# One more block group and one plain group less in both up projections, with a pinned order in the down projections

## The chip, the cores and the metric

The kernel runs on one core of one Trainium2 chip. The metric is the time of one execution on the device in microseconds; lower is better. The profile comes from one more execution of the same program, and its times count from the start of its span.

## The reference

A decoder trunk of two layers works on one sequence of 512 tokens with 1024 features, in float32. Layer 0 has an attention mixer, layer 1 a gated short convolution, and each layer ends with the same gated MLP, which is what the change touches:

```python
def conv_ffn(h, norm_g, w_up, conv_w, w_down):
    xn = rms_norm(h, norm_g)
    u = causal_dwconv(xn @ w_up, conv_w)      # width 3 along the tokens
    g, val = u[..., :D_FF], u[..., D_FF:]     # D_FF = 2816
    return (jax.nn.silu(g) * val) @ w_down
```

The up projection is 512 x 1024 times 1024 x 5632, the down projection 512 x 2816 times 2816 x 1024.

## The kernel before

**Precision.** Each float32 product is made of three matmuls on a fast float32 format. An operand is split into a high half `hi` (a copy by ScalarE into that format) and a low half `lo` (the rest, a subtraction on VectorE); hi x hi, hi x lo and lo x hi are summed in PSUM. So each block of weights that arrives costs one ScalarE copy (`whi`) and one VectorE subtraction (`wlo`) before TensorE can use it.

**Plain groups.** D_FF is cut into 22 column tiles of 128 for the gate and as many for the value; two neighbouring tiles make a group, of which there are `HF` = 11. The first `CLASSIC` = 3 groups of each MLP are multiplied plainly (`up_seven`, the loop over `j`): for each tile and each half (gate, value) `products` runs eight steps of three matmuls with 512 columns. They run on the activations before they are normalized, so this stage can start before the norm's row is known; `normed` multiplies the results by that row later.

**Block groups.** The other eight groups (class `Sevens`) use a seven-product scheme in the manner of Strassen: activations are cut into two halves of tokens and two of features, weights into four blocks of 512 x 256, and seven products of half size replace eight. `slot(g, s)` is one product of group `g` (24 matmuls with 256 columns, `seven`) with what is done beside it: weights are loaded (`load_pair`, `load_one`), summed on the way by accumulating transfers on the GpSimd queue (`add_block`) or by VectorE, split into halves (`weights_of`), and the results of the group before are joined, convolved, gated and multiplied (`tail`). The activations' seven forms are made once, by two runs of `prepare`, from the normalized rows.

**Chores.** Work that waits for the norm's row (`normed`, `prepare`, `gate_one`) is a list of generators. Between two steps of the plain stage, `work_off(SHARE)` gives the list a credit of 0.58 us and issues from it until the credit is used; each `yield` names a cost. What is left when the plain groups end is issued in the first block group, at 1.4 us per slot in its first four slots and without limit from the fifth on. `gate_one(g, i)` is the convolution (two VectorE taps for each half), SiLU and gate product of one tile of a plain group.

**Banks.** PSUM tiles have three tags: `a` (2 banks), `b` (4), `c` (2). A plain tile's gate half goes to `a`, its value half to `b`; block groups use `a` and `b`; the norm uses `c`.

**Down projection.** `mlp` runs 42 steps, seven phases (p1, p7, p2, p6, p3, q5, q4) over six groups of rows. Step `i` fetches the weights of step `i + 2`, multiplies, converts the activations of step `i + 2` (`operand`), and makes the block sums of step `i - 1` (`sums`). Weights of some phases are sums of two blocks: by accumulating transfers, or, for the last three groups of q5, by a second transfer into `other` and a VectorE sum (line 233).

**Order.** A scheduler orders the instructions of each engine ahead of time, by program order and by when it expects inputs to be ready; on the chip each engine but TensorE's weight loads takes its queue in that order. `tc.keep_in_program_order` ties an instruction behind the one traced just before it on its engine. Before the change it is used for the accumulating transfers and the `hi` copies of `weights_of`.

**The start.** `load(0)` brings the first 512 KB of attention weights in one transfer, queued on SyncE between the first and the second slice of x.

## Time and profile before

| | |
|---|---|
| median of 3 runs | 1135.77 us (1134.57 to 1136.08) |
| the profiled execution | 1138.21 us, span 1136.2 us |
| TensorE busy, share of the span | 1122.1 us, 99% |
| VectorE busy | 965.4 us, 85% |
| ScalarE busy | 670.3 us, 59% |
| first MLP: plain stage, block groups, down projection | from 278, 346.6 and 504 us |
| second MLP: the same | from 793, 861.7 and 1018 us |

How to read it: PE is TensorE, PEld its weight loads, DVE VectorE, ACT ScalarE, POOL GpSimd, SP SyncE. A timeline row gives the start and the duration in us, the engine, the line of the kernel, the operation, what it writes and reads, a count, and in brackets how long the engine was idle before it and what ended that. A row of windows gives a stretch, its length, busy time and count of each engine, then TensorE's granted clock, the transfer engines' share and GB/s.

### The profile page before, as it was taken

How to read it: one execution, taken by the hardware profiler on the slowest of the kernel's cores; microseconds unless marked ns; L12 is line 12 of the kernel's file. 1: busy time of each engine (PE TensorE's matmuls, PEld its weight loads, DVE VectorE, ACT ScalarE, POOL GpSimd, SP SyncE). 2: the span in 40 equal slices, each digit the busy share in tenths (PEclk: the TensorE clock that was granted, in tenths of full speed). 3: DMA queues.
4: the chain of work that ended last, by engine and by line, in shares of the span. 5: the costliest groups of instructions: out<-in, count | busy, mean ns of one | idle time of the engine just before them, and what ended most of it. 6: DMA issues, size and time to landing. Idle time of an engine off the chain costs nothing.

```text
span 1136.2 us, 19079 instructions
## 1 busy us (share of the span) xinstructions
PE 1122.1 (99%) x7547; PEld 1007.1 (89%) x7547; DVE 965.4 (85%) x1459; ACT 670.3 (59%) x999; POOL 133.0 (12%) x150
## 2 busy tenths in 40 slices
PE   8999999999999999999999999999999999999998
PEld 7888787878889999999999889988889999998886
DVE  6787888887899898989878888875798999889886
ACT  7556576755546767676547445544445766667553
POOL 4000000000012111014300001000001211014300
PEclk9999999999999999999999999999999999999999
DMA  6412212022366867689971655633375786789961
GB/s 192 112 38 75 57 39 74 26 87 75 106 182 118 191 160 163 172 235 194 224 185 31 172 118 142 130 111 93 93 195 112 167 191 137 181 220 216 230 168 56
DMA packets 160440, 155.31 MB, mean 137 GB/s; under 512 B 6396, under 2 KB 136492, under 8 KB 160352
## 3 DMA queue, kind: packets, MB, share of 16 engines
q1 hardware_dynamic: 124256, 106.94, 30.6%
q0 software_dynamic: 35936, 47.10, 25.1%
q8 instruction: 59, 0.97, 0.3%
q14 instruction: 29, 0.24, 0.1%
q10 hardware_dynamic: 160, 0.07, 0.0%
HBM read 149.10 MB, written 2.10 MB: 133 GB/s over the span
## 4 chain that ended last, share of the span: by engine, by line
PE 87%; DVE 6%; issue 2%; DMA 2%; ACT 2%; POOL 1%; DVEq 0%; SPq 0%; POOLq 0%; ACTq 0%
PE psb L1010 25%; PE psa L1010 10%; PE psb L1527 9%; PE psb L283 6%; PE psb L284 6%; PE psb L285 6%; PE psa L1527 6%; PE psa L285 4%; PE psa L283 4%; PE psa L284 4%; PE psb L658 1%; PE psa L754 1%; DMA raw<-in_ffn_w_down 1%; DVE rest L699 1%; DVE wlo L263 1%
## 5 line engine op out<-in xcount | busy, mean ns | idle before, releaser
L262 ACT ACTIVATE whi<-raw 128x1024 fp32r<-128x1024 f32 (+2 forms) x97 | 100.1, 1034 | 103.9 <-PE psb L284 31.9
L263 DVE TENSOR_TENSOR wlo<-raw,whi 128x1024 fp32r<-128x1024 f32 (+2 forms) x97 | 115.2, 1188 | 30.5 <-ACT whi L262 29.6
L1010 PE MATMUL psb<-p_hi,wlo_p 128*128 128x256 f32 x384 | 108.3, 282 | 0.6 <-DVE wlo_p L963 0.6
L1010 PE MATMUL psb<-p_lo,whi_p 128*128 128x256 f32 x384 | 108.1, 281 | 0.0
L1010 PE MATMUL psb<-p_hi,whi_p 128*128 128x256 f32 x384 | 107.8, 281 | 0.0
L283 PE MATMUL psb<-hs_a,whi 128*128 128x512 f32 x256 | 104.4, 409 | 0.0
L285 PE MATMUL psb<-hs_a,wlo 128*128 128x512 f32 x256 | 101.5, 397 | 0.0
L1010 PEld LDWEIGHTS psb<-p_hi,wlo_p 128*128 128x128 f32 x384 | 72.2, 188 | 0.8 <-DVE wlo_p L963 0.8
L1010 PEld LDWEIGHTS psb<-p_hi,whi_p 128*128 128x128 f32 x384 | 72.8, 190 | 0.0
L1010 PEld LDWEIGHTS psb<-p_lo,whi_p 128*128 128x128 f32 x384 | 72.3, 188 | 0.0
L1010 PE MATMUL psb<-q_hi,whi_q 128*128 128x256 f32 x256 | 72.0, 281 | 0.0
L1010 PE MATMUL psa<-p_lo,whi_p 128*128 128x256 f32 x256 | 72.0, 281 | 0.0
L1010 PE MATMUL psb<-q_lo,whi_q 128*128 128x256 f32 x256 | 72.0, 281 | 0.0
L1010 PE MATMUL psa<-p_hi,wlo_p 128*128 128x256 f32 x256 | 72.0, 281 | 0.0
L1010 PE MATMUL psb<-q_hi,wlo_q 128*128 128x256 f32 x256 | 72.0, 281 | 0.0
L1010 PE MATMUL psa<-p_hi,whi_p 128*128 128x256 f32 x256 | 71.8, 281 | 0.0
L1527 PE MATMUL psb<-act,whi 128*128 128x256 f32 x352 | 63.1, 282 | 0.0
L393 DVE SCALAR_TENSOR_TENSOR uv<-yv,taps,uv 128x511 f32<-128x511 f32 (+1 forms) x88 | 62.5, 744 | 0.2
L393 DVE SCALAR_TENSOR_TENSOR ug<-yg,taps,ug 128x511 f32<-128x511 f32 (+1 forms) x88 | 61.9, 743 | 0.3 <-ACT ug L390 0.3
L285 PEld LDWEIGHTS psb<-hs_a,wlo 128*128 128x128 f32 x256 | 48.1, 188 | 10.9
L283 PEld LDWEIGHTS psb<-hs_a,whi 128*128 128x128 f32 x256 | 48.4, 189 | 10.5 <-issue 1.2
L1527 PE MATMUL psb<-whi,act 128*128 128x512 f32 x176 | 56.7, 398 | 0.0
(458 smaller groups left out, 3645.7 us busy)
## 6 DMA issues: line engine op xcount, KB each, us to landing
raw<-in_attn_w_in SPq DMA_DIRECT2D x24, 512.0 KB, 4.0
raw<-in_ffn_w_up SPq DMA_DIRECT2D x24, 512.0 KB, 3.9
X<-in_ffn_w_up SPq DMA_DIRECT2D x16, 512.0 KB, 4.7
W<-in_ffn_w_up SPq DMA_DIRECT2D x16, 512.0 KB, 6.7
Y<-in_ffn_w_up SPq DMA_DIRECT2D x16, 512.0 KB, 4.5
Z<-in_ffn_w_up SPq DMA_DIRECT2D x16, 512.0 KB, 4.8
Y<-in_ffn_w_up POOLq DMA_DIRECT2D x16, 512.0 KB, 9.8
X<-in_ffn_w_up POOLq DMA_DIRECT2D x16, 512.0 KB, 7.4
```

The costliest lines, as they stand in the source:

```text
L262: return (act.activation(hi[:, at_], raw[:, at_], AF.Copy), dve.tensor_tensor(lo[:, at_], raw[:, at_], f32(hi[:, at_]), op=ALU.subtract))
L263: dve.tensor_tensor(lo[:, at_], raw[:, at_], f32(hi[:, at_]), op=ALU.subtract))
L283: made = [pe.matmul(acc, w[0], rhs[0], start=first, stop=False), pe.matmul(acc, w[0], rhs[1], start=False, stop=False), pe.matmul(acc, w[1 ...
L284: pe.matmul(acc, w[0], rhs[1], start=False, stop=False),
L285: pe.matmul(acc, w[1], rhs[0], start=False, stop=last)]
L393: dve.scalar_tensor_tensor(dst[:, d:], src[:, 0:S - d], tap(j), dst[:, d:], op0=ALU.mult, op1=ALU.add)
L658: pe.matmul(ss[e][:, c:c + wide], ql[rows, b * P:n], kl[rows, 0:wide], start=first and b == bs[0], stop=last and b == bs[-1])
L699: dve.tensor_tensor_scan(back, back, begin[:, S - n:S][:, ::-1], 0.0, op0=ALU.mult, op1=ALU.max)
L754: pe.matmul(out_, w, t[:, first:first + step * (NB - k - 1) + 1:step, :], start=k == 0 and i == 0, stop=k == NB - 1 and i == 1)
L1010: pe.matmul(to, w[a][:, k, c], x[b][:, k, :], start=fresh and i + k + t == 0, stop=i == 1 and k == 3 and t == 2, skip_group_check=not fresh)
L1527: pe.matmul(to, l, r, start=begin and o + t == 0, stop=end and t == 2 and o == (0 if layer else 1), skip_group_check=not fresh)
```

## The change

`CLASSIC` goes from 3 to 2: two plain groups and nine block groups. The chores are dealt out otherwise. In the plain stage only group 0's norm products and the two `prepare` runs are issued; gates and group 1's norm products follow in slices under the block groups, at 1.3 us per slot in the first, 1.0 in the first two slots of the second and 0.5 after that. Group 1's results wait in PSUM (banks b, b, c, c), and its gate works in a part of the memory that held the normalized halves. In the first block group the halves of p6 are made ahead of the copy of A. In the down projections the conversions (but for phase p1's), the block sums and the sums with `other` are tied behind the instruction traced before them. The first load of attention weights goes in two transfers.

```diff
-CLASSIC = 3
+CLASSIC = 2
...
-                dve.tensor_tensor(raw[:, 0:nk * n], raw[:, 0:nk * n], other[:, 0:nk * n], op=ALU.add)
+                pin(dve.tensor_tensor(raw[:, 0:nk * n], raw[:, 0:nk * n], other[:, 0:nk * n], op=ALU.add))
...
+            step = nk // 2 if i == 0 else nk
             for c0, width in zip(parts[::2], parts[1::2]):
-                with nc.allow_non_contiguous_dma(reason="eight columns"):
-                    nc.sync.dma_start(
-                        v[:, :, to:to + width], dram[k0 * P:(k0 + nk) * P, c0:c0 + width].rearrange("(k p) c -> p k c", p=P))
+                for k in range(0, nk, step):
+                    with nc.allow_non_contiguous_dma(reason="eight columns"):
+                        nc.sync.dma_start(
+                            v[:, k:k + step, to:to + width],
+                            dram[(k0 + k) * P:(k0 + k + step) * P, c0:c0 + width].rearrange("(k p) c -> p k c", p=P))
...
-    def halves_to(hi, lo, src, sign=1.0, held=False):
+    def halves_to(hi, lo, src, sign=1.0, held=()):
         made = act.activation(hi, src, AF.Copy, scale=sign)
...
+        for m, engine in ((made, "act"), (rest, "dve")):
+            if engine in held:
+                pin(m)
...
-            if g == self.groups[0]:
-                self.work_off(1.4 if s < 4 else 1e9)
+            if self.chores:
+                self.work_off(self.rate(g, s))
...
             elif s == 1:
+                if on and not was:
+                    self.weights_of(g, "p6", "Y")
                 if on:
                     act.activation(self.bank_of(g, "R"), c["A"], AF.Copy, scale=-1.0)
+                if on and was:
                     self.weights_of(g, "p6", "Y")
...
+        def wides_of(g):
+            if g == CLASSIC - 1:
+                t = hsp.tile([P, 8, S], F32, tag="hs_a", name=f"hs_a_wide{layer}")
+                return {n: t[:, 2 * i:2 * i + 2, :] for i, n in enumerate(("yg", "yv", "ug", "uv"))}
+            return {n: mp.tile([P, 2, S], F32, tag=n, name=f"{n}{layer}{g}", bufs=1) for n in ("yg", "yv", "ug", "uv")}
...
+        up.rate = lambda g, s: 1.3 if g == base else 1.0 if g == base + 1 and s < 2 else 0.5
...
-                accs.append(bank("ab"[half]))
+                accs.append(bank(("ab", "ab", "bb", "cc")[j][half]))
...
-            chores.append(normed(j // 2, j % 2, accs))
-            if j in (0, 2):
-                chores.append(prepare(j // 2))
-            for i in {1: (0, 1), 3: (2, 3), 4: (4,), 5: (5,)}.get(j, ()):
-                chores.append(gate_one(i // 2, i % 2))
+            kept.append(accs)
+            if j < 2:
+                chores.extend((normed(0, j, accs), prepare(j)))
+        chores.extend([gate_one(0, i) for i in range(2)] + [normed(1, i, kept[2 + i]) for i in range(2)] + [gate_one(1, i) for i in range(2)])
...
-            halves_to(t[:, 0, 0:nk, :], t[:, 1, 0:nk, :], blocks.block(name, k0, nk), sign)
+            halves_to(t[:, 0, 0:nk, :], t[:, 1, 0:nk, :], blocks.block(name, k0, nk), sign, held=("act", "dve") if p else ())
...
-                    dve.tensor_tensor(b, b, c, op=ALU.add)
+                    pin(dve.tensor_tensor(b, b, c, op=ALU.add))
...
-                    dve.tensor_tensor(a, b, a, op=ALU.subtract)
+                    pin(dve.tensor_tensor(a, b, a, op=ALU.subtract))
...
-                    dve.tensor_tensor(b, b, d, op=ALU.add)
+                    pin(dve.tensor_tensor(b, b, d, op=ALU.add))
```

`pin` is `tc.keep_in_program_order`.

More of the change, by code (lines that the diff above doesn't have):

```diff
@@ L218, in want_sum @@
         wanted.append((place, nk, n, blocks, queue))
-    brought = {}
+    brought, pin = {}, tc.keep_in_program_order
     def bring(i):
@@ L956, in trunk @@
     work_scope.close()
-    def halves_to(hi, lo, src, sign=1.0, held=False):
+    def halves_to(hi, lo, src, sign=1.0, held=()):
         made = act.activation(hi, src, AF.Copy, scale=sign)
-        if held:
-            tc.keep_in_program_order(made)
         if sign > 0:
-            dve.tensor_tensor(lo, src, f32(hi), op=ALU.subtract)
+            rest = dve.tensor_tensor(lo, src, f32(hi), op=ALU.subtract)
         else:
-            dve.scalar_tensor_tensor(lo, src, -1.0, f32(hi), op0=ALU.mult, op1=ALU.subtract)
+            rest = dve.scalar_tensor_tensor(lo, src, -1.0, f32(hi), op0=ALU.mult, op1=ALU.subtract)
+        for m, engine in ((made, "act"), (rest, "dve")):
+            if engine in held:
+                pin(m)
     LEFT, RIGHT = slice(0, HT), slice(HT, S)
@@ L1037, in weights_of @@
                 "p (k c) -> p k c", c=2 * P) for t in ("hi", "lo"))
-            halves_to(hi, lo, self.st[g][n], held=True)
+            halves_to(hi, lo, self.st[g][n], held=("act",))
             self.st[g][form] = hi, lo
@@ L1133, in trunk, with rate @@
         chores, credit, ahead = (), 0.0, False
+        def rate(self, g, s):
+            return 1.4 if s < 4 else 1e9
         def work_off(self, us):
@@ L1156, in up_seven @@
         up.norm, up.chores = norm, []
-        up.wides_of = lambda g: {n: mp.tile([P, 2, S], F32, tag=n, name=f"{n}{layer}{g}", bufs=1) for n in ("yg", "yv", "ug", "uv")}
+        def wides_of(g):
[3 more added lines that the diff above has]
+            return {n: mp.tile([P, 2, S], F32, tag=n, name=f"{n}{layer}{g}", bufs=1) for n in ("yg", "yv", "ug", "uv")}
+        up.wides_of = wides_of
         wides, forms, chores = up.wides, up.forms, up.chores
@@ L1211, in gate_one @@
             yield 0.86
+        kept = []
         for j in range(2 * CLASSIC):
```

## The prediction

> **What bounds the kernel now.** I read the page's first part, then its clock row, then the windows by stage, then the timeline of single engines where TensorE waits.
>
> ```profile
> PE 1122.1 (99%) x7547; PEld 1007.1 (89%) x7547; DVE 965.4 (85%) x1459; ACT 670.3 (59%) x999; POOL 133.0 (12%) x150
> PEclk9999999999999999999999999999999999999999
> 278.00:346.50 68.50, 68.50 (x302) 55.64 (x301) 63.21 (x104) 35.57 (x49) 3.80 (x3) 1.00 0.47 124
> 346.50:505.00 158.50, 157.88 (x1332) 157.47 (x1331) 143.65 (x172) 105.68 (x136) 26.96 (x22) 1.00 0.75 174
> ```
>
> TensorE is busy 99% of the span, and in the first MLP's plain stage (278 to 346.5) and block groups (346.5 to 505) it stands still for 0.62 us in all. So time comes out only if TensorE gets less to do, or if one of its few waits goes. VectorE is next, 63.2 of 68.5 and 143.7 of 158.5 us, and these are the stages that get more VectorE work in less time.
>
> **One plain group becomes one block group (both MLPs).** The plain group is four half tiles of 24 matmuls with 512 columns, the block group seven slots of 24 with 256.
>
> ```profile
> 290.29 0.39 PE L283 MATMUL psa<-hs_a,whi 128*128 128x512 f32 x1
> 341.00 0.39 PE L283 MATMUL psb<-hs_a,whi 128*128 128x512 f32 x1
> 346.60 0.28 PE L1010 MATMUL psa<-p_hi,whi_p 128*128 128x256 f32 x1
> ...
> 387.40 8.52 PE psb L1010 x72
> 466.93 8.52 PE psb L1010 x72
> ```
>
> The first two rows open the third and the twelfth half tile of a plain stage. The last one runs from 341.00 to 346.60, 5.60 us, and nine of them take 50.71 us with the norm's transposes among them, so 5.6 holds throughout; a plain group is 4 x 5.60 = 22.4 us. The last two rows, from the chain, stand at the same place of two block groups four apart: 79.53 / 4 = 19.88 us. The replacement saves 2.50 us of TensorE time in each MLP, **-5.0 us**. Both of these stages run at clock 1.00, so this is sure as far as TensorE is fed.
>
> **Feeding it: the VectorE ledger.** Durations, by start to start where VectorE works without a break, and where it idles:
>
> ```profile
> 405.07 0.68 DVE L1053 TENSOR_TENSOR yg<-psb,Xs 128x512 f32<-128x512 f32 x1
> 405.67 1.21 DVE L963 TENSOR_TENSOR wlo_p<-Z,whi_p 128x1024 fp32r<-128x1024 f32 x1
> 406.80 2.73 DVE L393 SCALAR_TENSOR_TENSOR ug<-yg,taps,ug 128x511 f32<-128x511 f32 x4
> 409.44 1.22 DVE L963 TENSOR_TENSOR wlo_p<-Y,whi_p 128x1024 fp32r<-128x1024 f32 x1
> ...
> 414.57 1.22 DVE L963 TENSOR_TENSOR wlo_q<-X,whi_q 128x1024 fp32r<-128x1024 f32 x1 [1.20 <-ACT whi_q L959]
> 413.03 0.28 PE L1010 MATMUL psb<-p_hi,wlo_p 128*128 128x256 f32 x1
> ```
>
> An operation on 512 elements takes 0.60 us, a weight half or a sum on 1024 takes 1.13, a convolution tap 2.64 / 4 = 0.66. A block group costs VectorE 7 weight halves and 2 sums (10.2), two joins and two products (2.4) and 8 taps (5.3): 17.9 of 19.88 us, and 1.2 of the rest it loses waiting for ScalarE (the row at 414.57). A plain group costs 4 weight halves, 4 norm products, 8 taps and four half-size gate products (0.34 each): 4.5 + 2.4 + 5.3 + 1.4 = 13.6. The change adds 4.3 us per MLP to VectorE and takes 2.5 us away from TensorE. The margin is in the last row: the p6 half that VectorE began at 409.44, and ended at 410.66, is first used at 413.03, a lead of 2.4 us.
>
> ```profile
> 293.66 0.69 DVE L1201 TENSOR_TENSOR yg<-psa,nrow_n 128x512 f32<-128x512 f32 x1 [1.09 <-ACT nrow_n L344]
> 347.06 1.22 DVE L1062 TENSOR_TENSOR Y<-Y,X 128x1024 f32<-128x1024 f32 x1
> ...
> 349.88 0.58 ACT L1098 ACTIVATE psb<-psa 128x512 f32<-128x512 f32 x1
> 350.39 1.04 ACT L959 ACTIVATE whi_p<-Y 128x1024 fp32r<-128x1024 f32 x1
> 353.29 0.39 PE L1010 MATMUL psb<-p_hi,wlo_p 128*128 128x256 f32 x1 [0.62 <-DVE wlo_p L963]
> ```
>
> In the first MLP the norm row is there at 293.66. The first block slot moves from 346.60 to about 324.2, which leaves 30.5 us. Before that slot VectorE must do both halves of `prepare` (each 4 scalings at 0.66 and 11 operations at 0.60: 9.26, so 18.5), four norm products (2.4), the remaining three plain weight halves (3.4), and p1, p7 and Y+X (3.4): 27.7 us. So 2.8 us are left for the first gate (4 taps and 2 half products, 3.3). What has not fitted of four gates and four norm products of group 1, 4 x 3.3 + 2.4 - 2.8 = 12.8 us, goes under the block groups. The first of these has six slots, 17.05 us, with 9.6 of its own (6 halves, 2 sums, a join), room 7.4; the second has room 2.0, of which 1.2 sits in that wait. By the new rates a tap pair and a gate's end (2.0) fall into the third. So 12.8 - 7.4 - 2.0 - 2.0 = 1.4 us of backlog stand against a lead of 2.4, and the third group's 2.0 fill its own room. TensorE should be nearly covered: I take **+0.9 us** in the first MLP (bounds 0, if the lead absorbs all, and 2.0, see the third case below). The second MLP has more slack:
>
> ```profile
> 806.01 0.69 DVE L1201 TENSOR_TENSOR yg<-psa,nrow_n 128x512 f32<-128x512 f32 x1 [2.23 <-ACT nrow_n L344]
> 861.89 2.85 PE psa L1010 x24
> ```
>
> From norm row to first block slot are 55.9 us against 52.9 in the first MLP, 3 us more, about one gate: **+0.2 us**. The transfers that a block group has beyond a plain one (two accumulating half megabytes) find the transfer engines at a 0.75 share in the block groups, with TensorE waiting for none of them; I cost them at nothing, and if q5's accumulated block came late, it would cost what is in the first MLP's bound.
>
> **p6's halves earlier in the first block group.** There no slot stands between p7 and p6, and p6's ScalarE half (350.39) is queued behind the copy of A (349.88), though its sum was ready at 348.3. The change puts it ahead of the copy. That is worth up to the 0.62 us wait above: **-0.6 us**, first MLP only. The copy is then 1 us later; its reader is the same p6 slot, and if that waits, the gain is 0.
>
> **Pinned order in the down projections.** Here the largest wait after the start stands:
>
> ```profile
> 582.15 0.69 DVE L233 TENSOR_TENSOR Y_chain<-Y_chain,other 128x512 f32<-128x512 f32 x1 [4.55 <-DMA other<-in_ffn_w_down]
> 582.76 1.22 DVE L263 TENSOR_TENSOR wlo<-raw,whi 128x1024 fp32r<-128x1024 f32 x1
> 579.26 1.06 ACT L262 ACTIVATE whi<-raw 128x1024 fp32r<-128x1024 f32 x1 [2.46 <-DMA raw<-in_ffn_w_down]
> 584.04 0.38 PE L1527 MATMUL psa<-act,wlo 128*128 128x256 f32 x1 [2.14 <-DVE wlo L263]
> 580.00:584.00 4.00, 1.90 (x17) 1.69 (x15) 1.84 (x3) 3.25 (x5) 0.00 (x0) 1.00 0.07 17
> 584.00:588.00 4.00, 3.96 (x20) 3.96 (x21) 4.00 (x6) 0.64 (x2) 0.00 (x0) 0.57 0.86 266
> ```
>
> VectorE holds at the sum Y_chain + other, whose transfer lands only at 582.1, and behind it in the queue stands the half that TensorE needs at 581.9. ScalarE had that half's partner done at 580.3, so without the sum in front it would be ready at 581.5. In the program the sum belongs to a step five later; pinned behind the joins and conversions traced ahead of it, it can't overtake. That removes 2.14 us, and with it what follows: clock 0.57 in the next 4 us, 0.43 x 4 = 1.7 us. **-3.8 us** (bounds 0 and -3.8).
>
> The Trainium skill (TensorE: Matmul & The Clock Gate, Part 1) has the clock halved only after an idle window of about 3.4 us. By that rule a wait of 2.14 us costs itself alone, and the sum below would be 1.7 us smaller. This trace shows clock 0.57 right behind a wait of 2.14, and I go by the row.
>
> A smaller case of the same kind:
>
> ```profile
> 528.72 1.06 ACT L262 ACTIVATE whi<-q_hi_chain 128x1024 fp32r<-128x1024 f32 x1 [1.86 <-PE psb L1527]
> 530.75 1.02 DVE L1428 TENSOR_TENSOR head<-head,hs_a_blocks 128x512 f32<-128x512 f32 x2
> 532.89 1.22 DVE L263 TENSOR_TENSOR wlo<-q_hi_chain,whi 128x1024 fp32r<-128x1024 f32 x1
> 534.16 0.39 PE L1527 MATMUL psb<-act,wlo 128*128 128x256 f32 x1 [0.76 <-DVE wlo L263]
> 1037.00:1050.00 13.00, 13.00 (x62) 10.40 (x61) 13.00 (x20) 8.30 (x13) 5.20 (x5) 1.00 1.07 183
> ```
>
> The half could start at 529.8 and started at 532.89, behind block sums of later steps. Pinned, these come behind. I take half of the 0.76, **-0.4 us** (bounds 0 and -0.8). In the same stretch of the second down projection VectorE is full too, yet TensorE isn't held (last row): 0 there, between -0.3 and the price in the second case.
>
> **First load in two transfers.** ScalarE waited 0.34 us for it, but TensorE's next wait, 0.32 us, is for a slice of x queued behind it:
>
> ```profile
> 6.43 0.63 ACT L262 ACTIVATE whi<-raw 128x512 fp32r<-128x512 f32 x1 [0.34 <-DMA raw<-in_attn_w_in]
> 8.39 0.86 PEld L826 LDWEIGHTS psb<-ident,x_tok 128*128 128x128 f32 x8 [0.32 <-DMA x_tok<-in_x]
> ```
>
> A second issue ahead of x gives back what the first half gains: 0, between -0.3 and +0.5.
>
> **Sum:** -5.0 + 0.9 + 0.2 - 0.6 - 3.8 - 0.4 = -8.7 us. The profiled execution took 1138.21 us (span 1136.2 and 2.0 around it), so it would become 1129.5. The median of the runs is 2.44 us below that execution: 1135.77 - 8.7 = **1127.1 us**.
>
> **Rivals.**
> First, *the wait in the first down projection stays*. The pinned sum only takes its place in the queue; the half itself isn't pinned, and ScalarE's half before it waited 2.46 us for its transfer, which landed 2.6 us before TensorE needed the product. If transfers are the limit there, or order stays as it is, both the 3.8 and the 0.4 fall away: -4.5, 1131.3 us. Against it: the half's inputs were complete at 580.3.
>
> Second, *slower: pinned conversions wait behind late transfers*.
>
> ```profile
> ACT whi L262 <- DMA raw<-in_ffn_w_down: 21.1, 9, 3.0
> ```
>
> Nine times ScalarE waited for down weights. Now conversions (0.60) and block sums (0.60) fill that gap on VectorE; pinned behind the weight half of their step, they come after it. A step then takes VectorE 1.13 + 0.6 + 0.6 = 2.3 us after the landing, against 2.8 us of TensorE. It decides once the half is already late by more than the 0.5 us of difference: then 1.2 us come on the path each time, 9 x 1.2 = 10.8. With all else as in the sum, -8.7 + 10.8 = +2.1, and a half-clock stretch of 1.7 after the longest: 1139.6 us. Against it: activations and weights of a step are needed together anyway, and in the block groups a pinned ScalarE half runs without loss.
>
> Third, *no change: VectorE becomes the bound under the first block groups*. If nothing is drawn forward into the plain stage, 15.6 us must go where 9.4 have room and 2.0 are put off: 4.2 us, less the lead of 2.4, is 1.8 us of wait, and with the half clock behind it (1.7) 3.5 in each MLP. That is -5.0 - 0.6 - 4.2 + 7.0 = -2.8, 1133.0 us; with half of the pins' 4.2 gone as well, 1135.1. I put this case at 1134.0 us. For it speaks that VectorE left p6 late in the first MLP already; against it, that it idled next to nowhere between 293.66 and 347.06 when work was there (63.2 of 68.5 us busy in the whole stage).
>
> **How the numbers follow.** The forecast has 0.62, the first rival 0.17, the third 0.12, the second 0.09. Forecast and first rival are faster; a measurement of this kernel can tell about 0.2% (2.3 us) from no change, so faster has 0.79, same 0.12, slower 0.09. The low end, 1124.5, takes every term at its good bound: no wait in the block groups (-1.1), the whole 0.76, the start and the second down projection 0.3 better each, which makes 1125.0, and half a microsecond between runs. The high end, 1133.0, takes in the first rival with 2.8 us of stalls in the place of 1.1 (1131.3 + 1.7), and leaves out the third for the most part and the second.
>
> **What would show it.** Right: block groups still 19.88 us apart, seven slots more of them, first slot near 324 and 839; no wait above 1 us in the first two groups of either MLP; the sum at line 233 behind the halves of the steps before, no row with a 2 us wait near 575 and no clock below 1.00 there. Wrong: TensorE waits on `wlo_p` or `wlo_q` in the second and third block groups, or ScalarE's halves standing behind a Silu that waits for taps; a wait in the down projections that ends with a conversion at line 963 or 965 instead of a weight half; a late first slice of x.

## The result, and the profile after

The changed kernel takes 1142.68 us, the median of 4 runs (1141.79 to 1143.22), beside 1135.92 us of the kernel before in the same session: ratio 1.0054, 95% interval [1.0042, 1.0067]. It is slower, by 0.5%; the prediction had 1127.1 us and a range that ended at 1133.0. The profiled execution took 1143.22 us (span 1141.5).

Stage lengths in us, each from TensorE's first product of a stage to its first of the next (timelines of TensorE), and what the prediction's terms would have made of each:

| stage | before | after | expected by the sum |
|---|---|---|---|
| start to the first plain stage | 278.3 | 279.8 | 278.3 |
| plain stage, first MLP | 68.3 | 46.0 | 45.9 |
| block groups, first MLP | 157.3 | **187.4** | 177.5 |
| down projection, first MLP | 118.6 | 112.7 | 114.4 |
| conv block and what lies between the MLPs | 170.9 | 172.2 | 170.9 |
| plain stage, second MLP | 68.4 | 46.0 | 46.0 |
| block groups, second MLP | 156.6 | 179.2 | 176.7 |
| down projection, second MLP | 113.8 | 113.6 | 113.8 |

The plain stages gave what was expected, and the first down projection more. All of the gain and some more went into the block groups of the first MLP. From the page of the changed kernel, its first part; from the windows by stage, the plain stage and the block groups of the first MLP, then the block groups of the second (columns: stretch, its length, busy time of TensorE, its weight loads, VectorE, ScalarE, GpSimd, then clock, DMA share, GB/s):

```profile
PE 1121.3 (98%) x7691; PEld 1011.9 (89%) x7691; DVE 973.4 (85%) x1461; ACT 677.3 (59%) x1013; POOL 137.9 (12%) x154
...
279.80:325.80 46.00, 46.00 (x206) 37.47 (x205) 41.76 (x71) 25.25 (x35) 1.40 (x1) 1.00 0.42 118
325.80:513.20 187.40, 181.43 (x1489) 178.73 (x1488) 169.28 (x205) 118.21 (x156) 32.01 (x26) 0.99 0.74 169
844.10:1023.00 178.90, 177.32 (x1490) 176.44 (x1489) 167.28 (x204) 118.60 (x157) 32.03 (x26) 1.00 0.74 173
```

The same products take 8.2 us longer in the first MLP than in the second (187.4 beside 179.2; the last row ends 0.4 us short of its stage). The chain of waits of the changed kernel, shares by line, names what is new:

```profile
PE psb L1014 16%; PE psb L1544 11%; PE psa L1544 8%; PE psa L1014 6%; DMA X<-in_ffn_w_up 6%; PE psb L286 5%; PE psb L287 5%; PE psb L288 5%; PE psa L286 2%; PE psa L288 2%; PE psa L287 2%; DVE wlo_p L964 2%; DMA Y<-in_ffn_w_up 2%; PE psa L757 2%; PE psb L661 2%
```

6% of 1141.5 us, some 68 us of the chain, lies in the accumulating transfers of X, the block whose halves q5 needs; some 40 of them are in the first MLP's block groups. A group of the first MLP in the timeline before, then the group with the longest wait for X but one in the timeline after, shows how it came onto the chain:

```profile
403.92 1.22 DVE L1062 TENSOR_TENSOR Y<-Y,X 128x1024 f32<-128x1024 f32 x1
405.69 1.30 POOL L1033 DMA_DIRECT2D X<-in_ffn_w_up  x1 [3.18 <-ACT whi_p L959]
409.62 1.07 ACT L1171 ACTIVATE ug<-ug 128x1024 f32<-128x1024 f32 x1 [0.74 <-DVE ug L393]
413.49 1.05 ACT L959 ACTIVATE whi_q<-X 128x1024 fp32r<-128x1024 f32 x1
415.85 0.60 ACT L1058 ACTIVATE Xs<-psb 128x512 f32<-128x512 f32 x1
433.38 1.05 ACT L959 ACTIVATE whi_q<-X 128x1024 fp32r<-128x1024 f32 x1
```

```profile
448.61 1.23 DVE L1066 TENSOR_TENSOR Y<-Y,X 128x1024 f32<-128x1024 f32 x1
450.37 1.29 POOL L1037 DMA_DIRECT2D X<-in_ffn_w_up  x1 [18.04 <-DVE Y L1066]
459.73 1.06 ACT L962 ACTIVATE whi_q<-X 128x1024 fp32r<-128x1024 f32 x1 [3.64 <-DMA X<-in_ffn_w_up]
460.69 1.05 ACT L1187 ACTIVATE ug<-ug 128x1024 f32<-128x1024 f32 x1
461.64 0.71 ACT L393 ACTIVATE uv<-yv,taps 128x512 f32<-128x512 f32 x1
462.25 0.58 ACT L1062 ACTIVATE Xs<-psb 128x512 f32<-128x512 f32 x1
462.88 0.39 PE L1014 MATMUL psb<-q_hi,whi_q 128*128 128x256 f32 x1 [1.27 <-ACT Xs L1062]
470.74 1.22 DVE L1066 TENSOR_TENSOR Y<-Y,X 128x1024 f32<-128x1024 f32 x1
480.07 1.06 ACT L962 ACTIVATE whi_q<-X 128x1024 fp32r<-128x1024 f32 x1 [1.86 <-DMA X<-in_ffn_w_up]
```

Before, Y+X ended at 405.1, X's transfer was issued at 405.7, and ScalarE took the half at 413.49 without waiting; so the next, 19.89 us later. After, from the issue at 450.37 to the half at 459.73 are 9.4 us, and ScalarE stands for 3.64 of them. Behind the half in its queue stand now Silu and a value tap, and only then the copy Xs, which empties the bank that q5's product goes into: TensorE waits for that copy. In the kernel before Silu stood ahead of the half (409.62), and Xs was done at 416.45, 2.0 us ahead of q5's slot (418.47). The late half also delays the work behind it for the next group, so that its Y+X comes at 470.74, 22.13 us behind 448.61. One lap of the chain, in the group before that one, shows the way round (rows of the chain, L1187 is Silu, the whi_q of 440.70 is q4's):

```profile
429.69 7.82 DMA X<-in_ffn_w_up
438.56 1.04 ACT ug L1187
440.70 0.96 ACT whi_q L962
441.71 1.22 DVE wlo_q L964
448.61 1.24 DVE Y L1066
450.37 9.28 DMA X<-in_ffn_w_up
```

It is a loop: the transfer of X, q5's half and what follows it in ScalarE's queue, then VectorE's queue with taps, products and the next group's low halves, Y+X, the next transfer. This lap took 20.68 us. Before, the loop had time over and TensorE set the step, but not much: by the trace of the kernel before, X landed 7.2 to 7.6 us behind its issue, 0.15 to 0.58 us ahead of the half, in the second to seventh group. After, groups three to eight take 20.4 to 22.2 us. The transfers are no slower on the whole (median from issue to landing 7.4 us before, 7.5 after); the two longest waits do stand behind the two longest of them, 9.28 and 9.87 us, and the last group's took 9.55 before as well.

ScalarE's order in one group of the kernel before was: gate taps, copy of A, p6's half, Silu, P7s, p2's half, q5's half, value taps, Xs. In the first MLP after it is: copy of A, a gate tap, p6's half, the other tap, P7s, p2's half, q5's half, Silu, a value tap, Xs, q4's half, the other value tap. The halves are pinned in the program, taps and Silu are not; no line of the change touches them. In the second MLP the old order is back from the third group on, and periods of 19.9 us from the fourth. There q5's half still waits for X, 0.4 to 1.7 us in eight of nine groups, and TensorE loses 0.5 us in the third group and 0.4 in the last: a wait of that size costs little where Xs doesn't stand behind Silu.

### The profile page after: what moved, and what is told of

It reads as the page before. It is cut to its first block, busy times and chain, and to the rows that moved or that the text cites. A ratio compares the mean times of both kernels' runs of the same rounds, so it can differ in the third digit from the quotient of the medians.

```text
span 1141.5 us, 19369 instructions
## 1 busy us (share of the span) xinstructions
PE 1121.3 (98%) x7691; PEld 1011.9 (89%) x7691; DVE 973.4 (85%) x1461; ACT 677.3 (59%) x1013; POOL 137.9 (12%) x154
## 4 chain that ended last, share of the span: by engine, by line
PE 74%; DVE 10%; DMA 8%; ACT 4%; issue 3%; SPq 0%; DVEq 0%; POOL 0%; POOLq 0%; ACTq 0%
PE psb L1014 16%; PE psb L1544 11%; PE psa L1544 8%; PE psa L1014 6%; DMA X<-in_ffn_w_up 6%; PE psb L286 5%; PE psb L287 5%; PE psb L288 5%; PE psa L286 2%; PE psa L288 2%; PE psa L287 2%; DVE wlo_p L964 2%; DMA Y<-in_ffn_w_up 2%; PE psa L757 2%; PE psb L661 2%
## 5 line engine op out<-in xcount | busy, mean ns | idle before, releaser
L1014 PE MATMUL psb<-p_hi,wlo_p 128*128 128x256 f32 x432 | 121.7, 282 | 0.2 <-DVE wlo_p L964 0.2
L1014 PE MATMUL psb<-p_lo,whi_p 128*128 128x256 f32 x432 | 121.6, 282 | 0.0
L1014 PE MATMUL psb<-p_hi,whi_p 128*128 128x256 f32 x432 | 121.3, 281 | 0.0
L286 PE MATMUL psb<-hs_a,whi 128*128 128x512 f32 x224 | 92.2, 412 | 0.0
L288 PE MATMUL psb<-hs_a,wlo 128*128 128x512 f32 x224 | 88.7, 397 | 0.0
L1014 PE MATMUL psb<-q_hi,whi_q 128*128 128x256 f32 x288 | 82.3, 286 | 4.8 <-ACT Xs L1062 4.6
L1014 PE MATMUL psa<-p_hi,wlo_p 128*128 128x256 f32 x288 | 82.1, 285 | 2.1 <-DVE wlo_p L964 1.9
L1014 PE MATMUL psb<-q_lo,whi_q 128*128 128x256 f32 x288 | 81.8, 284 | 0.0
L1014 PEld LDWEIGHTS psb<-q_hi,whi_q 128*128 128x128 f32 x288 | 55.2, 192 | 6.0 <-ACT Xs L1062 6.0
L1014 PEld LDWEIGHTS psa<-p_hi,wlo_p 128*128 128x128 f32 x288 | 54.1, 188 | 4.0 <-DVE wlo_p L964 3.8
```

The source lines that it names most:

```text
L286: made = [pe.matmul(acc, w[0], rhs[0], start=first, stop=False), pe.matmul(acc, w[0], rhs[1], start=False, stop=False), pe.matmul(acc, w[1 ...
L288: pe.matmul(acc, w[1], rhs[0], start=False, stop=last)]
L1014: pe.matmul(to, w[a][:, k, c], x[b][:, k, :], start=fresh and i + k + t == 0, stop=i == 1 and k == 3 and t == 2, skip_group_check=not fresh)
```

## The experiments

| kernel | ratio to before | 95% interval | block groups, first MLP | second MLP | first down |
|---|---|---|---|---|---|
| after | 1.0054 | 1.0042 to 1.0067 | 187.4 | 179.2 | 112.7 |
| e1_late_before | 1.0034 | 1.0022 to 1.0045 | 163.5 (eight groups) | 156.5 | 114.1 |
| e2_early_after | 0.9977 | 0.9967 to 0.9986 | 179.9 | 178.4 | 113.9 |
| e3_pins_alone | 0.9973 | 0.9963 to 0.9984 | 157.6 (eight groups) | 156.7 | 113.2 |
| e4_early_clean | 0.9952 | 0.9938 to 0.9967 | 178.8 | 178.8 | 113.0 |
| e5_no_gate_backlog | 0.9951 | 0.9938 to 0.9964 | 176.8 | 178.3 | 112.8 |
| e6_early_fixed | 0.9964 | 0.9952 to 0.9976 | 178.3 | 178.8 | 112.7 |
| e7_split_alone | 1.0013 | 1.0002 to 1.0025 | 157.6 (eight groups) | 156.5 | 116.2 |
| e8_clean_no_pins | 0.9966 | 0.9954 to 0.9978 | 178.7 | 178.1 | 114.3 |
| e9_q5_without_sum | 0.9960 | 0.9946 to 0.9974 | 176.8 | 179.1 | 113.0 |
| e10_fine_slices | 0.9976 | 0.9966 to 0.9986 | 179.2 | 178.9 | 113.0 |
| e11_fine_slices_all | 0.9959 | 0.9945 to 0.9972 | 177.9 | 178.3 | 112.7 |
| e12_q5_last | 0.9949 | 0.9936 to 0.9963 | 177.3 | 177.8 | 113.3 |

Lengths are those of the profiled execution, taken as above. Nine groups without a stall would take 157.3 + 19.88 = 177.2 us in the first MLP and 176.5 in the second.

**The order alone, put into the kernel before.** e1 pins the tail's taps and Silu where they are traced, in the first MLP, which puts them behind the halves:

```diff
+                tc.keep_in_program_order(act.activation(dst[:, i, :], src[:, i, :], AF.Copy, scale=taps_of(g, half, i)(2)))
...
-                act.activation(wides[p]["ug"], wides[p]["ug"], AF.Silu)
+                made = act.activation(wides[p]["ug"], wides[p]["ug"], AF.Silu)
+                if late:
+                    tc.keep_in_program_order(made)
```

> The kernel before, with three plain groups and all gates in the plain stage; only in the first MLP's block groups the tail's ScalarE work is tied to its place in the program, so that the second gate tile's first tap stands behind p6's half and SiLU and the value taps stand behind q5's half, as they stand after the change. If this order is what lengthens each block group (order theory), the groups of the first MLP are about 20.4 to 21.5 us apart instead of 19.88, 4 to 10 us in all, and the kernel takes 1139 to 1146 us. If the gate slices push VectorE behind and the groups never catch up (backlog theory), nothing is pushed here: 19.88 us a group and 1136 us.

Its block stage grew by 6.2 us and the time by 3.9 us (0.34% of 1136.9). The timeline of ScalarE in e1, q5's half in two groups:

```profile
435.42 1.06 ACT L959 ACTIVATE whi_q<-X 128x1024 fp32r<-128x1024 f32 x1 [2.02 <-DMA X<-in_ffn_w_up]
455.92 1.06 ACT L959 ACTIVATE whi_q<-X 128x1024 fp32r<-128x1024 f32 x1 [2.01 <-DMA X<-in_ffn_w_up]
```

They are 20.50 us apart, with a wait for X that the kernel before has not. From the second group to the seventh the halves follow each other in 20.5 to 20.7 us. TensorE still steps in 19.95 to 19.97 us up to the fourth group, and from the fifth on in 20.5 to 20.6 too. So the long order is enough to make the loop bind, without any of the change's work. Of the 6.2 us 4.0 lie in the last group, where TensorE waits 1.82 us behind the copy Xs and its clock then falls, as it does in the changed kernel's last group.

**The order undone in the changed kernel.** e2 moves the tail forward by a slot, so that taps and Silu are traced ahead of the halves that they must not hold:

```diff
-            if s < 2:
-                conv(p, 0, s)
-            elif s == 3:
+            if s == 0:
+                conv(p, 0, 0)
+                conv(p, 0, 1)
+            elif s == 1:
                 act.activation(wides[p]["ug"], wides[p]["ug"], AF.Silu)
+            elif s == 3:
                 conv(p, 1, 0)
-            elif s == 4:
                 conv(p, 1, 1)
```

> The kernel after, with the block groups' tail traced earlier in the program (both gate taps in the first slot, SiLU in the second, both value taps in the fourth), so that from the fourth block group on the instructions stand as they did before the change; the gate slices stay. Order theory: waits only in the first three block groups of the first MLP, 19.88 us a group after that, about 6 to 8 us less than after the change, 1135 to 1137 us. Backlog theory: the groups stay at 20.4 us and more, and the time within 2 us of after, 1141 to 1143 us.

The ratio fell from 1.0054 to 0.9977, 8.7 us; 7.5 of it is the first MLP's block stage, of which 4.0 in the last group. The groups from the fifth on were 19.95 us, the second to the fourth still 20.7 to 21.2.

**The loop cut.** e9 is the changed kernel with its long order and all its work; only q5's halves are made from W in both MLPs, so that nothing waits for the transfer of X and q5 multiplies another matrix:

```diff
-                    self.weights_of(g, "q5", "X")
+                    self.weights_of(g, "q5", "X" if self.ahead else "W")
```

> The changed kernel, with q5's weight halves in both MLPs made from W, the block that p2 has just used, in place of the accumulated X; every instruction and transfer stays, X's accumulating transfer too, only nobody in the loop waits for it (what q5 multiplies is another matrix). ScalarE's static order is unchanged, the long one in the first MLP. Theory A (the loop q5 half, taps and Silu, next group's halves, Y+X, accumulating transfer of X, q5 half is longer than 19.88 us): without the wait for X the groups of the first MLP after the third are 19.9 to 20.3 in place of 20.4 to 22.2, the first block stage goes from 187.4 to about 180, and the time from 1142.7 to about 1135. Theory B (the order alone holds ScalarE's halves behind Silu and taps, whatever X does): groups stay at 20.4 to 22, time 1142 within 1.

Theory A held, and by more than it asked for: 176.8 us, all steady groups at 19.95 or 19.96, the early ones among them; the ratio fell from 1.0054 to 0.9960, 10.7 us. The windows of e9, the third group of the first MLP (VectorE without a free moment) and the whole stage up to its last group's end:

```profile
364.00:384.00 20.00, 20.00 (x171) 20.00 (x170) 20.00 (x29) 13.11 (x17) 6.77 (x6) 1.00 0.88 188
...
326.90:503.70 176.80, 176.80 (x1489) 176.76 (x1488) 168.89 (x205) 118.51 (x156) 29.56 (x24) 1.00 0.75 173
```

TensorE is busy in all of the 176.8 us, with the same VectorE work (168.89 beside 169.28 us) and with Silu still behind q5's half from the third group on. In the changed kernel, then, neither the order nor the work holds TensorE by itself; they do it by way of the wait for X.

**The put-off gate work.** e4 is e2 with one first load again and the conv block's p6 half behind its copy, as before:

```diff
-            step = nk // 2 if i == 0 else nk
+            step = nk
...
-                if on and not was:
+                if on and not was and not self.ahead:
                     self.weights_of(g, "p6", "Y")
...
-                if on and was:
+                if on and (was or self.ahead):
```

> As the second run, with the first load in one transfer again and p6's half behind the copy again in the short convolution's block groups. If the start's +1.5 us and the short convolution's +1.3 us of after come from these two edits, it takes 2.8 us less than the second run, and the order theory puts it at 1132 to 1134 us. If they come from something else, the second and fourth runs take the same time.

It reached 1132.15 us, ahead of both kernels. Three of its groups in the first MLP still took 20.75, 21.12 and 20.27 us. Two kernels on top of it ask whether work or order does that. e5 leaves out VectorE's taps of group 1's gates, and so a part of the computation:

```diff
-                conv(g, half, i)
-                yield 1.5
+                if g:
+                    act.activation(u[half][:, i, :], wides[g][("yg", "yv")[half]][:, i, :], AF.Copy, scale=taps_of(g, half, i)(2))
+                else:
+                    conv(g, half, i)
+                    yield 1.5
```

> As e4, but the eight convolution taps on VectorE of plain group 1's two gates are left out (each gate's output starts from its first tap on ScalarE alone), 5.3 us of VectorE work per MLP that in e4 lies under the first block groups. ScalarE's static order in the second and third block group of the first MLP is still the long one (p6's half ahead of the gate taps). Theory A (work put off fills VectorE): groups of 20.75, 21.12 and 20.27 us in e4's first MLP become 19.9 to 20.1, some 2.2 us less; the first group of the second MLP, 18.8 in e4, goes to about 17.5; in all -3 us on e4's 1132.2, 1129. Theory B (only the order makes those groups long): they stay at 20.5 to 21.2, and the time at 1132 within 0.7.

All steady groups came to 19.96 us (theory A there), but the first group of the second MLP did not shorten (19.26), and in time e5 can't be told from e4 (0.9951 beside 0.9952). e6 pins taps, Silu and the copy of A in the good order and keeps the work:

```diff
+                pin(act.activation(dst[:, i, :], src[:, i, :], AF.Copy, scale=taps_of(g, half, i)(2)))
...
-                act.activation(wides[p]["ug"], wides[p]["ug"], AF.Silu)
+                pin(act.activation(wides[p]["ug"], wides[p]["ug"], AF.Silu))
...
+                    if was and not self.ahead:
+                        pin(made)
```

> As e4, with ScalarE's order fixed in all block groups: both gate taps, then the copy of A, then p6's half, then Silu. All the put-off gate work stays. Theory A: the second to fourth group of the first MLP stay at 20.3 to 21.1 us, since VectorE is full there; time as e4's, 1132 within 0.7. Theory B: they fall to 19.9 to 20.1, 2.2 us less, 1130.

Groups of 20.67 and 21.26 us stayed, the fourth fell to 19.88: mostly theory A. In the early groups the work, not ScalarE's order, costs the time. It does so in two ways. The timeline of e4 has, for the second group, VectorE's low half of q4 and TensorE's wait for it, then q5's half of the third and fourth group:

```profile
358.23 1.21 DVE L964 TENSOR_TENSOR wlo_q<-Y,whi_q 128x1024 fp32r<-128x1024 f32 x1
359.50 0.39 PE L1014 MATMUL psb<-q_hi,wlo_q 128*128 128x256 f32 x1 [0.59 <-DVE wlo_q L964]
...
373.81 1.06 ACT L962 ACTIVATE whi_q<-X 128x1024 fp32r<-128x1024 f32 x1 [2.25 <-DMA X<-in_ffn_w_up]
394.75 1.06 ACT L962 ACTIVATE whi_q<-X 128x1024 fp32r<-128x1024 f32 x1 [2.08 <-DMA X<-in_ffn_w_up]
```

In the third and fourth group the wait for X is the longest of that stage. In the second group q5's half, at 352.47, did not wait for X at all: VectorE worked without a break and had four value taps ahead of q4's low half. So there the put-off work holds TensorE by VectorE's queue alone. e9 has 19.96 us in that group too, but its value taps stand behind q4's low half for the most part; whether the place of the taps or the earlier half brought that, no run separates.

**The work in thinner slices.** e10 and e11 are e6 with single taps and lower credit; e11 drops the two slots at 1.0 too:

```diff
-                conv(g, half, i)
-                yield 1.5
+                for j in (1, 0):
+                    d = 2 - j
+                    dve.scalar_tensor_tensor(dst[:, i, d:], src[:, i, 0:S - d], taps_of(g, half, i)(j), dst[:, i, d:], op0=ALU.mult, op1=ALU.add)
+                    yield 0.75
...
-        up.rate = lambda g, s: 1.3 if g == base else 1.0 if g == base + 1 and s < 2 else 0.5
+        up.rate = lambda g, s: 1.3 if g == base else 1.0 if g == base + 1 and s < 2 else 0.28
```

> As e6, with the gates' taps handed out one at a time and 0.28 us of credit a slot (1.96 a group, the room that a block group has) from the second block group's third slot on, in place of pairs at 0.5 (3.5 a group). Theory A (the groups at 20.3 to 21.3 us carry more put-off work than they have room for): spread thinner, groups two to four come to 20.0 to 20.5, and 1 to 2 us are gained on e4, 1130.5 to 1131. Theory B (the work has no room in any group, as 1.2 us of each is lost to waits for ScalarE): the same 2.3 us are lost over more groups, 1132.

> As e10, with 0.28 us of credit from the second block group's first slot on, so that the two slots at 1.0 fall away too. Theory A: the second group, 20.7 in e6, comes to about 20, 1130. Theory B: as e10, 1132; or worse, if the norm products of group 1, which hold accumulators in psb and psc, are late for p7 of a later group: then a wait of TensorE for psb stands at its start.

e10 missed theory A: the long groups only moved, to 21.31 and 21.03 us one place later, and the time with them (0.9976). In e11 the groups took 20.57, 19.86 and 20.95, which misses theory A too; its interval overlaps e4's. Handing the work out thinner gained nothing that can be told from e4.

**The loop given a slot more.** e12 is e4 with q4 ahead of q5:

```diff
-                              ("q5", "R", False), ("q4", "T", False))[s]
+                              *((("q5", "R", False), ("q4", "T", False))[::1 if self.ahead else -1]))[s]
...
-                    self.weights_of(g, "q5", "X")
+                    self.weights_of(g, *(("q5", "X") if self.ahead else ("q4", "Y")))
...
```

> As e4, with q4 and q5 changed over in the MLPs' block groups: q4, which needs no accumulated X, in the sixth slot, q5 in the seventh, and the two joins changed over with them (yg behind q4, yv in the next group's first slot). Each transfer of X then has one slot, 2.84 us, more to land. Theory A (the loop through X's accumulating transfer is what made the first groups of e4 20.3 to 21.1 us, and e9 without it had 19.96): every steady group 19.9 to 20.0, the first block stage 177 in place of 178.8, the second 178.3 or less, 1130 in all. Theory B (the put-off gate work fills VectorE in the first groups, whatever X does): 178.8 stays, 1132. If the later yv join makes the value taps late, waits of TensorE for psb or wlo_q stand in every group, and it is slower than e4.

The wait for X is gone from all nine of its halves, and the first MLP's stage came to 177.3 us with groups of 19.89, 20.55 and 19.96 in the place of 20.75, 21.12 and 20.27, as theory A said for the most part. Of the stage's 1.5 us little can be told in the time: 1131.17 us and 0.9949 beside e4's 0.9952. It is the fastest kernel here, with all of the computation, though not told apart from e4.

**The pins.** e3 is the kernel before with the pins of both down projections and nothing else, e8 is e4 without them:

```diff
-            halves_to(t[:, 0, 0:nk, :], t[:, 1, 0:nk, :], blocks.block(name, k0, nk), sign)
+            halves_to(t[:, 0, 0:nk, :], t[:, 1, 0:nk, :], blocks.block(name, k0, nk), sign, held=("act", "dve") if p else ())
...
-                    dve.tensor_tensor(b, b, c, op=ALU.add)
+                    pin(dve.tensor_tensor(b, b, c, op=ALU.add))
...
```

> The kernel before with the pinned order in the down projections and nothing else. If the pins gained what the stage lengths say (first down projection 118.6 us before, 112.7 after), this takes 1130 us (-5.9), without the 2.14 us wait at the sum of Y_chain and without the clock drop behind it. If the shorter stage came from its later or different start, with the pins moving the wait only, 1134 to 1136 us.

> As e4, without the pins of the down projections. Theory A (the pins take the 2 us wait out of the first down projection, and the wait of 1.1 us for p6's half in the conv stage came with them): down0 goes from 113.0 to about 118.5, the row with a wait of about 2 us is back behind the sum at line 233, the conv stage falls from 125.8 to 124.6; in all +4.3, 1136.5, ratio about 0.999. Theory B (the two plain groups and the order under the block groups already move that sum): down0 stays within 1 us of 113, 1132 within 1. Theory C for the conv stage: its 1.1 us stay at 125.8 without the pins, since they come from the copy and the half there.

In e3 the down projection fell by 5.4 us and the time by 3.1 (0.27% of 1136, interval 1.8 to 4.2), about half of the 5.9 expected by the stage lengths. e8 missed: 114.3 where theory A asked for 118.5. But its timeline shows the wait that the pins remove, VectorE's row of the sum and TensorE's behind it:

```profile
578.04 0.69 DVE L233 TENSOR_TENSOR Y_chain<-Y_chain,other 128x512 f32<-128x512 f32 x1 [3.89 <-DMA other<-in_ffn_w_down]
578.64 1.22 DVE L266 TENSOR_TENSOR wlo<-raw,whi 128x1024 fp32r<-128x1024 f32 x1
579.92 0.39 PE L1545 MATMUL psa<-act,wlo 128*128 128x256 f32 x1 [1.47 <-DVE wlo L266]
...
576.00:580.00 4.00, 2.53 (x22) 2.32 (x20) 1.96 (x3) 4.00 (x6) 0.00 (x0) 1.00 0.27 90
580.00:584.00 4.00, 4.00 (x34) 4.00 (x35) 4.00 (x6) 1.85 (x4) 0.00 (x0) 1.00 0.84 268
```

In the timeline of the changed kernel the same sum has no wait in front and comes 12 us after the place where it used to hold VectorE:

```profile
577.03 1.22 DVE L266 TENSOR_TENSOR wlo<-raw,whi 128x1024 fp32r<-128x1024 f32 x1
...
594.82 0.68 DVE L233 TENSOR_TENSOR Y_chain<-Y_chain,other 128x512 f32<-128x512 f32 x1
```

So the pins do what the prediction said. What they are worth hangs on the length of the wait: 2.14 us with the clock at 0.57 behind it in the profiled execution of the kernel before, 1.65 us and no clock loss in e7, 1.47 in e8, 1.21 in e1, which has no pins in the down projections either. Without them the stage took 118.6, 116.2, 114.3 and 114.1 us in these four profiled executions, with them 112.7 to 113.9 in all the others. In time e4 and e8 are 1.6 us apart (0.14% of 1136.8), with intervals that overlap.

**The first load in two.** e7 is the kernel before with that edit alone:

```diff
+            step = nk // 2 if i == 0 else nk
...
+                for k in range(0, nk, step):
```

> The kernel before, with only the first load of the first product in two transfers. Theory A (the split costs the start): the first plain stage opens at 279.4 to 279.8 in place of 278.3, and the time is 1.1 to 1.5 us longer, ratio 1.0010 to 1.0013. Theory B (the later start in the changed kernel's profiled execution was that execution's own, as e2, with the split, opened the stage at 278.6): 278.3 to 278.6, ratio 1.0000 to 1.0003.

The ratio, 1.0013, came out as theory A said; the stage opened 0.9 us later, at 279.2. TensorE's and ScalarE's rows in e7:

```profile
7.51 0.63 ACT L265 ACTIVATE whi<-raw 128x512 fp32r<-128x512 f32 x1 [0.55 <-DMA raw<-in_attn_w_in]
9.14 1.09 PE L829 MATMUL psb<-ident,x_tok 128*128 128x128 f32 x8 [1.31 <-DMA x_tok<-in_x]
```

The wait for the first slice of x was 0.32 us before and is 1.31 here (1.12 in the changed kernel); the second half of the load is waited for too. e2, with the split, opened the stage at 278.6, and e9, with it too, at 280.9; kernels without it opened it at 277.7 to 279.0. So the price differs from execution to execution, and the 0.9 us of one profile would not show it alone.

## Why the prediction was wrong

**TensorE's work, -5.0: right.** The plain stages lost 22.3 and 22.4 us, and e9 shows the eight groups behind the first at 19.95 us and no stall in the first MLP.

**Feeding it, +0.9 and +0.2: this step failed.** Measured against 177.2 and 176.5 us it is +10.2 in the first MLP (+11.0 without the gain of p6 below) and +2.7 in the second. The prediction counted VectorE's work in a ledger and set 1.4 us of backlog against a lead of 2.4. The ledger was near enough: VectorE is full in e9's third group too, where TensorE loses nothing. Its sum did leave out what e4's second group shows, that the order within a full queue matters. What it priced at nothing stands in one of its sentences: the transfers "find the transfer engines at a 0.75 share in the block groups, with TensorE waiting for none of them; I cost them at nothing, and if q5's accumulated block came late, it would cost what is in the first MLP's bound". It did come late, and the bound, 2.0 us, was for one backlog worked off once. The wait for X closes a loop from group to group, so that a delay isn't worked off but paid again: eight of nine of q5's halves in the first MLP waited for X, where the kernel before has six of eight without. The lead that counted was not VectorE's 2.4 us but the 0.15 to 0.58 us between X's landing and the half. The prediction had the place under its eyes: VectorE's low half at 414.57, read as room lost, stands behind the half that ScalarE began at 413.49, 0.27 us after X had landed.

The second failure is that the unpinned part of a queue can come out in another order. The prediction named "ScalarE's halves standing behind a Silu that waits for taps" among the signs of being wrong, and gave it no price. Here the Silu waited for nothing; it stood between q5's half and the copy Xs. e1 and e2 put 6.2 and 7.5 us on the order in the first MLP's stage, 4.0 of each in the last group with the clock's fall behind its long wait; the put-off work is most of the rest (2.0 us between e4 and e5).

In the second MLP 1.8 of the 2.7 us lie in the first group, 19.0 us beside 17.2 before; the third and the last take 0.5 and 0.4 more. The timeline of the changed kernel there:

```profile
851.66 0.68 DVE L1218 TENSOR_TENSOR hs_a_wide<-psb,nrow_n 128x512 f32<-128x512 f32 x1
852.26 1.28 DVE L1218 TENSOR_TENSOR hs_a_wide<-psc,nrow_n 128x512 f32<-128x512 f32 x2
853.32 0.38 PE L1014 MATMUL psa<-p_hi,whi_p 128*128 128x256 f32 x1 [0.49 <-ACT whi_p L962]
853.46 1.22 DVE L964 TENSOR_TENSOR wlo_p<-W,whi_p 128x1024 fp32r<-128x1024 f32 x1
854.73 0.38 PE L1014 MATMUL psa<-p_hi,wlo_p 128*128 128x256 f32 x1 [0.58 <-DVE wlo_p L964]
```

Group 1's norm products stand ahead of p2's half. That fits a backlog of norm products and group 0's gates, which e5 left in place; no run took these away, so it stays argued.

**p6 earlier, -0.6: right in size.** The first group of the first MLP went from 17.93 to 17.12 us, 0.8 less, and the wait of 0.62 us is gone; no run has this edit alone.

**The pins, -4.2: right in mechanism.** The down projection lost 5.9 us between the two profiled executions. By the runs e3 has -3.1. The clock's share of the price, 1.7 us, belonged to that execution and not to each: e1 and e7, without pins, kept the clock there. The runs beside e3 fit that: of 22 of the kernel before, five have a mean clock of 0.998 and a median of 1138.35 us, fourteen have 1.000 and 1136.59; of e3's eight, one has 0.998.

**The first load, 0: too low.** +1.5 us between the two profiles, +0.13% by e7 (interval 0.02 to 0.25%); the bound was +0.5.

**The conv block, not in the sum: +1.3.** Its program is as before but for p6's half, and e3 and e4, without that edit there, lose 0.8 and 1.1 us, with 0.95 and 0.94 us of wait for p6's half. VectorE's order moved by one instruction, first before, then after, in the timelines:

```profile
668.12 1.22 DVE L1062 TENSOR_TENSOR Yc<-Yc,Xc 128x1024 f32<-128x1024 f32 x1
668.78 0.28 PE L1010 MATMUL psa<-p_hic,whi_p1c 128*128 128x256 f32 x1
669.25 0.68 DVE L1339 TENSOR_TENSOR early_lo<-psb,nrow_n 128x512 f32<-128x512 f32 x1
```

```profile
672.13 0.28 PE L1014 MATMUL psa<-p_hic,whi_p1c 128*128 128x256 f32 x1
672.33 0.69 DVE L1356 TENSOR_TENSOR early_lo<-psb,nrow_n 128x512 f32<-128x512 f32 x1 [0.28 <-PE psb L288]
672.93 1.22 DVE L1066 TENSOR_TENSOR Yc<-Yc,Xc 128x1024 f32<-128x1024 f32 x1
679.18 0.38 PE L1014 MATMUL psb<-p_hic,wlo_p6c 128*128 128x256 f32 x1 [0.93 <-DVE wlo_p6c L964]
```

Before, Yc+Xc ran 0.7 us ahead of the first block slot; after, it stands behind a product that waits for the last plain tile, and p6's half is 1 us late. e3 has nothing but the pins of the down projections and has this order too; e8, without them, has the old one. So the pins moved an instruction in a stage that they don't touch. In e8 a like loss came at q5's slot instead, a wait of 0.92 us, so theory C there held in size and not in place.

The terms as measured, with -0.2 for the second down projection, are +1.5 - 4.9 + 11.0 - 0.8 + 2.7 - 5.9 - 0.2 + 1.3 = +4.7, against 5.0 between the two executions (1143.22 - 1138.21). The medians lie 6.8 apart, since the profiled execution of the kernel before was 2.3 us above its median and that after 0.5.

**The rivals.** The third had the right place and the right sign of the mechanism, work put off that makes the block groups late, but it too priced a backlog that ends: 1134.0. The first fell with e3. The second fell with the changed kernel itself: in its first down projection TensorE has no stall above 0.4 us. Its sign, a wait that ends with a conversion, stands once in e2 (0.56 us at 580.91).

## What to carry to other kernels

When a stage gets fuller, look for loops that run from one group to the next through a transfer, and compare the loop's length, queue by queue, with the step of the bounding engine; a loop that just fits has no lead to spend, and a delay in it is paid in every group. Where only some instructions of a queue are pinned, the rest may come out in another order after a change elsewhere, here in a stage that the diff didn't touch; compare the order of each engine's queue, group by group, as soon as both kernels are there. Giving the consumer of an accumulating transfer the last slot of its group took the wait away here (e12), though the time can't be told from e4's; copies that empty a bank belong ahead of what isn't urgent.

## What was not expected of the hardware

Inside the MLPs the clock fell only behind the longer stalls of TensorE. Behind 1.27 us at 462.88 in the changed kernel, 1.65 in e7 and 1.47 in e8 it stayed at 1.00; behind the 1.82 us of e1 and the 1.85 us at 505.94 in the changed kernel it fell, as behind the 2.14 us of the kernel before. The timeline and windows of the changed kernel:

```profile
505.94 0.39 PE L1014 MATMUL psb<-q_hi,whi_q 128*128 128x256 f32 x1 [1.85 <-ACT Xs L1062]
503.80:507.80 4.00, 2.15 (x16) 1.94 (x15) 3.56 (x4) 4.00 (x7) 1.58 (x2) 0.93 1.02 361
507.80:511.80 4.00, 4.00 (x25) 4.00 (x24) 4.00 (x8) 3.90 (x7) 0.85 (x1) 0.64 0.97 170
```

So a stall of 1.85 us cost 1.7 us more: 0.07 x 4 + 0.36 x 4. Among these stalls the line runs between 1.65 and 1.82 us. That is no rule for the chip: at the start of e9 the clock fell too, behind two waits of 0.60 and 0.69 us, as its window shows, and no run varied the length of a stall alone.

```profile
9.86:13.27 3.41, 3.41 (x14) 2.99 (x13) 2.10 (x3) 1.98 (x4) 0.00 (x0) 0.50 1.14 317
```

The Trainium skill (TensorE: Matmul & The Clock Gate, Part 1) puts the fall behind an idle window of about 3.4 us, which these runs do not bear out.
